# A third Strassen product taken by a second level in the second feed-forward product of a transformer layer; its weight differences made in an earlier stage

## The chip, the core and the metric

The kernel runs on one core of a Trainium2 chip. The metric is the device time of one execution in microseconds (us). A core has TensorE (PE, with its weight load PEld), VectorE (DVE), ScalarE (ACT), GpSimd (POOL), and SyncE (SP), which here issues nearly all DMA transfers. Each engine runs its instructions in the order in which the program lists them, and waits on semaphores for the others.

## What is computed

One layer of a transformer trunk, in float32, for x of 1024 x 1024 (sequence by model width), memory of 256 x 1024, and a feed-forward width of 4096. Cut to what matters:

```
h = rmsnorm(x, g_mix_pre);  proj = h @ w_in
y = concat(rmsnorm(forgetting_attention(...)), rmsnorm(chunked_relpos_attention(...)))
x = x + rmsnorm(y @ w_out, g_mix_post)
h = rmsnorm(x, g_mem_pre);  mem_n = rmsnorm(mem, g_mem_kv)
y = memory_cross_attention(h, mem_n, w_mq, w_mk, w_mv, w_mo)      # 4 heads
x = x + rmsnorm(y, g_mem_post)
h = rmsnorm(x, g_ff_pre)
y = square(relu(h @ w_ff1)) @ w_ff2                               # 1024x1024x4096, 1024x4096x1024
x = x + rmsnorm(y, g_ff_post)
```

## The kernel before

Every float32 operand is split into a high part (rounded, on ACT, `whi`, `ah`, ...) and a low part (the rest, mostly on DVE, `wlo`, `al`, ...), and every product is three matmuls: high by high, high by low, low by high. The large products use Strassen's scheme with seven products of half-size blocks, in the variant whose right-hand differences are T1 = B12 − B11, T2 = B22 − T1, T3 = B22 − B12 and T4 = T2 − B21 (the signs are carried by the sums).

The stages, by their time in the profiled execution:

- **Attention**, to about 500 us.
- **The memory attention stage**, about 500 to 816 us: the output projection of the attention, the memory queries, scores, and the product with `w_mo`. Its order is not written out: a planner (class `Flow`) takes steps for TensorE from several generators, and keeps for V (VectorE), S (ScalarE), G (GpSimd) and D (the DMA queue) a clock of its own and a list of waiting pieces, each with a cost in us and a level. A piece with a lower level goes first. "Pumps" are called ahead of each step and may put new pieces into the lists. A load is reckoned to take 4.5 us (3.5 in `Sums`) after its 0.55 us of issue. One pump, `Sums` (L1095 to L1124), already makes right-hand differences: it loads pieces of `w_mo`, forms T1 to T4 on DVE (`B11r`, `B12r`, ..., L1115) and stores them to DRAM. The order that the planner finds is the order of each engine's instructions.
- **The tail of that stage**, about 816 to 838 us, ordered by hand: the last column of the product with `w_mo` (`ym11b`), while DVE makes the last low parts `wlomo_1_2` and `wlomo_1_3` (L455) and POOL adds rows (`xf`).
- **The first feed-forward product**, to 1147.9 us: for 16 blocks j of 256 columns of the hidden layer, one Strassen level, order written out by hand. A block adds its weight pieces (`Weights.sums`, `sum4`: `sd`), splits them (`v0lo_s`, ...), runs products into the banks px, pz, pv, and turns the sums into seven left-hand matrices for the second product, stored in DRAM (`put(j, n, ...)` into `gd`). For j < 7 a first half of the block was computed in advance and is read back (`p1r`). In `if late` (0 < j < 7) the next block's weight sums are on DVE, otherwise on POOL. The matrices n = 1 and n = 5 are stored in parts (`put_parts`), and after each odd j a "form" per matrix (`put_sums`, four DVE instructions of 128x256, L1893 and on, and two stores) makes the sums S1 to S4 of a second level. The forms are made in the next block, one after `g22` (`g<-pz,u`) and one at its end.
- **The second feed-forward product**, from 1147.9 us to about 1447: Strassen with seven products n, eight "outer" steps k each. An outer step is 24 matmuls of 128x512 into four banks. n = 1 and n = 5 are taken by a second Strassen level, 14 "inner" steps each, an inner step being 24 matmuls of 128x256 (bank `fi`). n = 3 (T1) comes first, by eight outer steps into banks of its own (`fy`); then n = 0, 2, 4, 6 into `fx`, with one inner step after each outer step (and a second one at four places) until all 28 are done. So there are 68 steps. `fetch` loads a step's two operands four steps ahead, `combine` (L2186 to L2215) forms its right-hand difference on DVE, and `prepare` (L2217 to L2234) splits both operands (L2229 to L2232).

Of the kernel before, what the change touches and what calls it, by code (L numbers as in the profile page):

```python
# [14 lines left out]
F32 = mybir.dt.float32  # L15
# [120 lines left out]
def build(ctx, tc, nc, out, t):  # L136
# [119 lines left out]
    p1 = pool("p1", stack=p1s)  # L256

# [83 lines left out]
    def value_leave(g, kb, ps):  # L341
# [12 lines left out]
        if g == 0:  # L354
# [9 lines left out]
                 q=4, mp=4, pt=1, xt=2, wq=0).items()}  # L364
# [760 lines left out]

    class Rows:
# [646 lines left out]
    p2x = pool("p2x", stack=p2xs)  # L1773
    with tc.manual_schedule():
# [4 lines left out]
        flow.pumps.append(Sums().pump)  # L1779
# [17 lines left out]
    NP = FF // (2 * P)  # L1797
# [7 lines left out]
    def t2(name):  # L1805
        if region[0]:
            return pr.tile([P, HT], F32, tag="t2", bufs=9, name=name)
        return pf.tile([P, HT], F32, tag="t2", bufs=18, name=name)
# [62 lines left out]
    HQ = HT // 2  # L1871
    gi, even = {}, {}
    for n in (1, 5):
# [15 lines left out]
    def put_sums(n, j, c):  # L1889

        k, s, e = j // 2 % 4, j // 8, even.pop(n)
# [251 lines left out]

    NK = NP // 2
    W11, W12, W21, W22 = range(4)
    order = ((0, "B11"), (1, "B21"), (4, "T2"), (3, "T1"), (5, "T3"), (6, "B22"), (2, "T4"))
    inner = ("A11", "A12", "S2", "S1", "S3", "S4", "A22")
    steps, i = [(3, k) for k in range(NK)], 0
    for m, n in enumerate((0, 2, 4, 6)):
        for k in range(NK):  # L2150
            steps.append((n, k))
            for _ in range(min(28 - i, 1 + (m * NK + k in (6, 11, 14, 17)))):
                steps.append((("i", i // 14), i % 14))
                i += 1
    rows_a, rows_b, ops = {}, {}, {}
    t1, t2b = {}, {}

    def raw_b(q, k):
        r = u4(f"wg{q}_{k}_{len(rows_b)}", (P, D), F32)
        nc.sync.dma_start(r, t["w_ff2"][q, k])  # L2160
        return r

    def fetch(s):
# [4 lines left out]
        if n in (("i", 0), ("i", 1)):  # L2168
            name, h = inner[k // 2], k % 2
            nc.sync.dma_start(ra, gi[(1, 5)[n[1]], name][h].rearrange("p a b -> p (a b)"))  # L2170
            quads = {"A11": (0, 1), "A12": (2,), "S2": (3,), "S1": (), "S3": (0,), "S4": (3,), "A22": (2,)}[name]
            rows_b[s] = []
            for q in quads:
                rows_b[s].append(u4(f"wi{q}_{s}", (P, D), F32))
                nc.sync.dma_start(rows_b[s][-1], t["w_ff2q"][n[1], q, h])
# [3 lines left out]
        if name == "T1":  # L2179
            rows_b[s] = (raw_b(W12, k), raw_b(W11, k))  # L2180
        else:
            rows_b[s] = (raw_b({"B11": W11, "T2": W22, "T3": W11, "T4": W21}[name], k),)
# [3 lines left out]
    def combine(s, eng=nc.vector):  # L2186
# [3 lines left out]
        if isinstance(n, tuple):  # L2190
            name, key = inner[k // 2], ("i", k % 2)
            if name == "A11":
                t1[key] = rb[1]
                eng.tensor_sub(rb[1], rb[1], rb[0])
            elif name == "S1":
                rb = (t1.pop(key),)
            elif name == "S2":
                t2b[key] = rb[0]
                eng.tensor_sub(rb[0], rb[0], t1[key])
            elif name == "S3":  # L2200
                eng.tensor_sub(rb[0], t2b[key], rb[0])
            elif name == "A22":
                eng.tensor_sub(rb[0], rb[0], t2b[key])
        elif n == 3:
            t1[k] = rb[0]
            eng.tensor_sub(t1[k], *rb)
        elif n == 2:
            t2b[k] = t1.pop(k)
            eng.tensor_sub(t2b[k], rb[0], t2b[k])
            rb = (t2b[k],)  # L2210
        elif n == 4:
            eng.tensor_sub(rb[0], t2b[k], rb[0])
        elif n == 6:
            eng.tensor_sub(rb[0], rb[0], t2b[k])
# [20 lines left out]
    with manual:  # L2235
        sums, stores = (lambda: []), []
        for j in range(NP):
# [3 lines left out]
            late = more and 0 < j < AHEAD  # L2241
# [25 lines left out]
            forms = sums()  # L2267
# [19 lines left out]
            stores = [form() for form in forms[:1]]  # L2287
            if late:
# [25 lines left out]
            stores = [form() for form in forms[1:]]  # L2314
# [4 lines left out]
            def sums(j=j, u2=u2, u3=u3, g11=g11, g22=g22):  # L2319
# [4 lines left out]
                put(j, 3, s1)  # L2324
# [6 lines left out]
                return [lambda: put_sums(1, j, u3), lambda: put_sums(5, j, s4g)] if j % 2 else []  # L2331
# [260 lines left out]
```

## Time and profile before

| | us |
|---|---|
| Median of 3 runs | 1458.01 (1457.24 to 1458.23) |
| Profiled execution, its time | 1455.46 |
| Profiled execution, its span | 1453.7 |
| TensorE busy | 1443.0 (99%) |
| First matmul of the first feed-forward product's block loop | 880.4 |
| First matmul of the second feed-forward product | 1147.9 |

The span runs from the first to the last instruction of the profile; 1.8 us of the time lie outside it. The profile lists busy time by engine, waits by what ended them, groups of equal instructions, and single instructions with start and duration. A row of the timeline reads: start, duration, engine, line, operation, output<-inputs, shape, and in brackets the idle time ahead of it with what ended it. Rows of several instructions end in x and their count.

### The profile page before, as it was taken

The numbers are of one execution on the slowest core, as the hardware profiler recorded it, in microseconds if no ns is written. First come the engines' busy times: TensorE is split into PE (matmuls) and PEld (weight loads), VectorE is DVE, ScalarE is ACT, GpSimd is POOL, SyncE is SP. The second block draws the span as 40 slices with busy tenths as digits, with TensorE's granted clock in tenths as the row PEclk, the third lists the DMA queues.
The fourth block names the chain that finished last, engine by engine and source line by source line (L and its number), as shares of the span: only waits on it lengthen the run. The fifth ranks groups of instructions, "written<-read, shape, count | busy, mean of one in ns | idle before, by whom it ended". The sixth has DMA issues, their size and how long they took to land.

```text
span 1453.7 us, 21860 instructions
## 1 busy us (share of the span) xinstructions
PE 1443.0 (99%) x7553; PEld 1231.0 (85%) x7553; DVE 1093.1 (75%) x1854; ACT 845.1 (58%) x1465; POOL 389.1 (27%) x496
## 2 busy tenths in 40 slices
PE   9999999999999999999999999999999999999998
PEld 8988888888889888888788888888888888888886
DVE  7787777766677847976874687896666866789897
ACT  6567677666677836555553455555555545555553
POOL 1245456554455311521231411003223000000003
PEclk9999999999999999999999999999999999999999
DMA  7132324321325585552541546875545897786786
GB/s 277 49 97 71 83 64 144 86 81 48 95 58 154 175 307 181 188 177 85 178 155 44 177 154 222 278 251 182 177 167 188 309 342 247 253 281 231 278 288 204
DMA packets 104351, 255.29 MB, mean 176 GB/s; under 512 B 11673, under 2 KB 30113, under 8 KB 104241
## 3 DMA queue, kind: packets, MB, share of 16 engines
q1 hardware_dynamic: 104096, 253.65, 52.7%
q8 instruction: 59, 0.97, 0.3%
q14 instruction: 52, 0.42, 0.1%
q10 hardware_dynamic: 144, 0.26, 0.1%
HBM read 184.07 MB, written 61.40 MB: 169 GB/s over the span
## 4 chain that ended last, share of the span: by engine, by line
PE 96%; DVE 2%; ACT 1%; issue 0%; DMA 0%; SPq 0%; DVEq 0%; ACTq 0%
PE pv L754 4%; PE fx L194 4%; PE fx L193 4%; PE fx L195 4%; PE ptr L711 4%; PE px L195 3%; PE px L194 3%; PE px L193 3%; PE pz L193 2%; PE k L193 2%; PE mq L195 2%; PE q L193 2%; PE q L194 2%; PE q L195 2%; PE mq L194 2%; PE k L194 2%
## 5 line engine op out<-in xcount | busy, mean ns | idle before, releaser
L717 DVE TENSOR_TENSOR phl<-ptr,phl 128x512 fp32r<-128x512 f32 (+1 forms) x152 | 92.5, 615 | 31.6 <-ACT phl L720 30.6
L720 ACT ACTIVATE phl<-ptr 128x512 fp32r<-128x512 f32 (+1 forms) x152 | 79.7, 539 | 40.4 <-PE ptr L711 38.6
L2229 ACT ACTIVATE whif<-ra 128x1024 fp32r<-128x1024 f32 x45 | 47.6, 1058 | 77.7 <-PE fx L194 34.8
L2364 POOL TENSOR_SCALAR rf<-sf 128x1 f32<-128x1 f32 x7 | 7.0, 1001 | 315.8 <-ACT jf L2345 315.6
L754 PE MATMUL pv<-phl,vs 128*128 128x512 f32 (+1 forms) x304 | 85.2, 366 | 0.2 <-DVE phl L717 0.2
L2231 DVE TENSOR_TENSOR wlof<-ra,whif 128x1024 fp32r<-128x1024 f32 x45 | 54.9, 1221 | 36.0 <-ACT whif L2229 35.8
L193 PE MATMUL fx<-vhif,whif 128*128 128x512 f32 x168 | 65.6, 390 | 0.0
L194 PE MATMUL fx<-vlof,whif 128*128 128x512 f32 x168 | 65.6, 390 | 0.0
L195 PE MATMUL fx<-vhif,wlof 128*128 128x512 f32 x168 | 65.4, 389 | 0.0
L754 PEld LDWEIGHTS pv<-phl,vs 128*128 128x128 f32 x304 | 55.1, 188 | 11.1 <-DVE phl L717 0.8
L768 POOL TENSOR_TENSOR o<-o 64x256 f32<-64x256 f32 x64 | 47.8, 747 | 52.8 <-DVE o L766 34.4
L2080 POOL TENSOR_TENSOR sc<-wf,wf 128x512 f32<-128x512 f32 x8 | 12.7, 1589 | 176.9 <-DMA wf<-in_w_ff 163.3
L766 DVE TENSOR_TENSOR o<-pv,o 64x512 f32<-64x512 f32 x64 | 44.0, 688 | 13.6 <-ACT o L771 12.2
L193 PE MATMUL k<-hT_hi,whik 128*128 128x512 f32 x128 | 53.6, 419 | 0.0
L193 PE MATMUL q<-hT_hi,whiq 128*128 128x512 f32 x128 | 51.6, 403 | 0.0
L193 PE MATMUL mq<-h2T_hi,whimq 128*128 128x512 f32 x128 | 51.3, 401 | 0.0
L195 PE MATMUL k<-hT_hi,wlok 128*128 128x512 f32 x128 | 50.3, 393 | 0.0
L195 PE MATMUL mq<-h2T_hi,wlomq 128*128 128x512 f32 x128 | 50.1, 392 | 0.2 <-DVE wlomq L455 0.2
L194 PE MATMUL k<-hT_lo,whik 128*128 128x512 f32 x128 | 50.3, 393 | 0.0
L195 PE MATMUL q<-hT_hi,wloq 128*128 128x512 f32 x128 | 50.2, 392 | 0.0
L194 PE MATMUL q<-hT_lo,whiq 128*128 128x512 f32 x128 | 50.2, 392 | 0.0
L194 PE MATMUL mq<-h2T_lo,whimq 128*128 128x512 f32 x128 | 50.1, 392 | 0.1
(715 smaller groups left out, 5207.7 us busy)
## 6 DMA issues: line engine op xcount, KB each, us to landing
wg<-in_w_ff SPq DMA_DIRECT2D x48, 512.0 KB, 6.0
ra<-gd SPq DMA_DIRECT2D x40, 512.0 KB, 4.8
wf<-in_w_ff SPq DMA_DIRECT2D x38, 512.0 KB, 4.2
wi<-in_w_ff2q SPq DMA_DIRECT2D x28, 512.0 KB, 6.4
wrawmq<-in_w_mq SPq DMA_DIRECT2D x16, 512.0 KB, 4.1
gd<-s SPq DMA_DIRECT2D x32, 256.0 KB, 2.6
gd<-g SPq DMA_DIRECT2D x25, 256.0 KB, 2.7
wrawq<-in_w_qk SPq DMA_DIRECT2D x8, 512.0 KB, 4.6
```

The costliest lines, as they stand in the source:

```text
L193: nc.tensor.matmul(ps, lh, rh, start=start, stop=False, skip_group_check=more)
L194: nc.tensor.matmul(ps, lh, rl, start=False, stop=False, skip_group_check=more)
L195: nc.tensor.matmul(ps, ll, rh, start=False, stop=stop, skip_group_check=more)
L711: nc.tensor.transpose(tr[:, m, :], sp[:, k * P:(k + 1) * P], ident)
L717: flow.put("V", at, 0.7, lambda: nc.vector.tensor_sub(pl[:, live, :], tr[:, live, :], f(ph[:, live, :])), done)
L720: flow.put("S", flow.end, 0.6, lambda ph=ph, tr=tr, live=live: nc.scalar.activation(ph[:, live, :], tr[:, live, :], AF.Copy), split)
L754: nc.tensor.matmul(pv[:, :, qs_, :], v, hl[:, :, hs, :], start=c == 0 and turn == 0, stop=last)
L766: flow.put("V", at, 0.7, lambda: nc.vector.tensor_add(o2[own], pv[own, :, :, ::step], o2[own]), lambda end: (free["pv"].give(end), flow.pu ...
L768: free["pv"].give(end), flow.put("G", end, 0.8, lambda: nc.gpsimd.tensor_add(o2[own, 0], o2[own, 0], o2[own, 1]), store)))
L2080: eng.tensor_sub(sc[:, k1], r0[:, k0], r1[:, k0])
L2229: nc.scalar.activation(ah, ra, AF.Copy)
L2231: nc.vector.tensor_sub(al, ra, f(ah))
```

## The change

Three parts.

**In the memory attention stage** a new pump, `Ready`, works off 16 units (eight k, two column halves a) between 60 and 400 us of the planner's time after the stage's start. A unit takes four buffers of 128x512 of a new pool `pp` (eight buffers), loads one piece of each quadrant of `w_ff2`, makes four differences on DVE at level 3 (behind everything else that is ready), and stores them: T3 to `wd[4]`, T1 to `t1d`, T2 to `wd[2]`, T4 to `wd[6]`. Together 64 DVE instructions and 128 transfers of 256 KB.

**In the first feed-forward product** the matrix n = 3 is stored in parts and gets forms as n = 1 and n = 5 have. The three forms of two blocks wait in a queue: in each block one is made after `g22`, and at the end of a block half of what is left. `late` now ends one block earlier (0 < j < 6), so at j = 6 the weight sums of the next block are on POOL. The forms of the last block are made in steps 2, 4 and 6 of the second product.

**In the second feed-forward product** n = 3 is taken by 14 inner steps, ahead of those of n = 1 and n = 5. There are 32 outer and 42 inner steps, 74 in all: from the second outer step on two inner steps follow each outer one, and the last eight outer steps are alone. Outer steps load their right-hand difference ready-made (`wd`), and the inner steps of n = 3 load theirs from `t1d` in runs of 1 KB. The DVE combinations of the outer steps are gone; those of the inner steps stay.

```diff
+    START, WHEN = [], ((60, 400),)
+    class Ready:
...
+        def pump(self):
+            if self.left and free["pp"].ready(4) and any(x <= flow.now - START[0] < y for x, y in WHEN):
+                for _ in range(4):
+                    free["pp"].take()
+                self.unit(*self.left.pop(0))
+        def unit(self, k, a):
+            r, lv = {}, 3
...
+            def load(q, then):
+                flow.load(flow.now, lambda: nc.sync.dma_start(r[q], t["w_ff2"][q, k][:, cs]), then)
+            def sub(op, x, y, z):
+                return [("V", 0.6, lambda: op(r[x], r[y], r[z]))]
...
+            last = lambda at: flow.chain(at, sub(minus, W21, W21, W11), made(W21, whole(6)), lv)
+            t2_ = lambda at: flow.chain(at, sub(plus, W11, W22, W11), made(W11, whole(2), last), lv)
+            t1_ = lambda at: flow.chain(at, sub(minus, W12, W12, W11), made(W12, t1d[k // 4][:, k % 4, a], t2_), lv)
+            landed = all_of(("pp", k, a), 4, lambda at: flow.chain(at, sub(minus, W22, W22, W12), made(W22, whole(4), t1_), lv))
...
-        flow.pumps.append(Sums().pump)
+        flow.pumps += [Sums().pump, Ready().pump]
+        START.append(flow.now)
...
-    for n in (1, 5):
+    for n in (1, 5, 3):
...
-    steps, i = [(3, k) for k in range(NK)], 0
+    steps, i = [], 0
     for m, n in enumerate((0, 2, 4, 6)):
         for k in range(NK):
             steps.append((n, k))
-            for _ in range(min(28 - i, 1 + (m * NK + k in (6, 11, 14, 17)))):
-                steps.append((("i", i // 14), i % 14))
+            w = m * NK + k
+            while i < min(42, 42 * (w - 1) // 22):
+                steps.append((("i", (2, 0, 1)[i // 14]), i % 14))
                 i += 1
...
+                if n[1] < 2:
+                    nc.sync.dma_start(rows_b[s][-1], t["w_ff2q"][n[1], q, h])
+                else:
+                    nc.sync.dma_start(rows_b[s][-1].rearrange("p (a n) -> p a n", a=4),
+                                      t1d[h][:, :, q // 2, q % 2 * HQ:q % 2 * HQ + HQ])
...
+        right[s] = u4(f"wg{s}", (P, D), F32)
+        nc.sync.dma_start(right[s], t["w_ff2"][W11, k] if n == 0 else wd[n][k])
...
-            late = more and 0 < j < AHEAD
+            late = more and 0 < j < AHEAD - 1
...
-            forms = sums()
+            forms += sums()
...
             stores = [form() for form in forms[:1]]
+            del forms[:1]
...
-            stores = [form() for form in forms[1:]]
+            stores = [form() for form in forms[:len(forms) // 2]]
+            del forms[:len(forms) // 2]
...
-                put(j, 3, s1)
+                put_parts(3, j, s1)
```

What the engines' rows show. First VectorE at the end of the memory attention stage, before (L455 makes a low part, L1565 scales a row of `ym`):

```order
L455 TENSOR_TENSOR wlomo_1_0_9206<-wrawmo_1_0_9001,whimo_1_0_9205 128x1024
L455 TENSOR_TENSOR wlomo_1_1_9225<-wrawmo_1_1_9180,whimo_1_1_9224 128x1024
L1565 TENSOR_TENSOR ym_9035<-ym_9043,g_mem_post 128x512
L1565 TENSOR_TENSOR ym_9036<-ym_9051,g_mem_post 128x512
L1565 TENSOR_TENSOR ym_9037<-ym_9129,g_mem_post 128x512
L455 TENSOR_TENSOR wlomo_1_2_9261<-wrawmo_1_2_9216,whimo_1_2_9260 128x1024
L1565 TENSOR_TENSOR ym_9038<-ym_9143,g_mem_post 128x512
L455 TENSOR_TENSOR wlomo_1_3_9271<-wrawmo_1_3_9228,whimo_1_3_9270 128x1024
```

The same place in the change, where L1156 with `pp` is a unit's difference:

```order
L461 TENSOR_TENSOR wlomo_1_1_9495<-wrawmo_1_1_9429,whimo_1_1_9494 128x1024
L1156 TENSOR_TENSOR pp_71_9433<-pp_71_9433,pp_71_9431 128x512
L1156 TENSOR_TENSOR pp_71_9431<-pp_71_9431,pp_71_9432 128x512
L1156 TENSOR_TENSOR pp_71_9432<-pp_71_9433,pp_71_9432 128x512
L1614 TENSOR_TENSOR ym_9273<-ym_9281,g_mem_post 128x512
L1156 TENSOR_TENSOR pp_71_9434<-pp_71_9434,pp_71_9432 128x512
L1614 TENSOR_TENSOR ym_9274<-ym_9292,g_mem_post 128x512
L461 TENSOR_TENSOR wlomo_1_2_9536<-wrawmo_1_2_9486,whimo_1_2_9535 128x1024
L1614 TENSOR_TENSOR ym_9275<-ym_9384,g_mem_post 128x512
L1614 TENSOR_TENSOR ym_9276<-ym_9396,g_mem_post 128x512
L461 TENSOR_TENSOR wlomo_1_3_9552<-wrawmo_1_3_9498,whimo_1_3_9551 128x1024
```

The last unit's four differences now stand behind `wlomo_1_1` and ahead of `wlomo_1_2`.

Second, VectorE in block j = 5 of the first feed-forward product, before:

```order
L2282 TENSOR_TENSOR u_5_10643<-px_10583,p1r_10528 128x512
L2286 TENSOR_TENSOR g_5_10645<-pz_10614,u_5_10643 128x512
L2087 TENSOR_TENSOR sd_10647<-wf_10448,sc_10627 128x512
L1848 TENSOR_TENSOR v0lo_s_10650<-sc_10627,v0hi_s_10649 128x1024
L1848 TENSOR_TENSOR wlo_s1a_10671<-wf_10526,whi_s1a_10670 128x1024
```

And in the change (`s_33` are the tiles of the new form):

```order
L2315 TENSOR_TENSOR u_5_10945<-px_10885,p1r_10830 128x512
L2319 TENSOR_TENSOR g_5_10947<-pz_10916,u_5_10945 128x512
L1942 TENSOR_TENSOR s_33_10949<-s_2_10644,s_3_10769 128x256
L1943 TENSOR_TENSOR s_33_10949<-s_33_10949,s_2_10644 128x256
L1944 TENSOR_TENSOR s_33_10950<-s_2_10644 128x256
L1945 TENSOR_TENSOR s_33_10950<-s_3_10769,s_33_10949 128x256
L2136 TENSOR_TENSOR sd_10955<-wf_10750,sc_10929 128x512
L1898 TENSOR_TENSOR v0lo_s_10958<-sc_10929,v0hi_s_10957 128x1024
```

The four instructions of the form for n = 3 have come between `g` and the next block's `sd` and low part.

Third, the DMA issues on SP in the second feed-forward product, before (`gd` and `gi` hold left-hand matrices, `in_w_ff` and `in_w_ff2q` are the weights):

```order
L2178 DMA ra_12442<-gd_0_9276 128x1024
L2160 DMA wg_0_1_12444<-in_w_ff 128x1024
L2170 DMA ra_12479<-gi1A_9342 128x1024
L2175 DMA wi_9_12481<-in_w_ff2q 128x1024
L2175 DMA wi_9_12483<-in_w_ff2q 128x1024
```

And in the change:

```order
L2213 DMA ra_13161<-gi3S_9650 128x1024
L2221 DMA wi_18_13163<-t1d_156 128x4x256
L2225 DMA ra_13206<-gd_0_9594 128x1024
L2227 DMA wg_13208<-wd_0_132 128x1024
L2213 DMA ra_13242<-gi3S_9651 128x1024
L2221 DMA wi_20_13244<-t1d_157 128x4x256
L2213 DMA ra_13282<-gi3A_9646 128x1024
L2221 DMA wi_21_13284<-t1d_156 128x4x256
```

Two inner steps, reading `gi3` and `t1d`, now stand between two outer steps, and an outer step reads `wd`.

118 lines of the change are left out of this document (56 added, 62 removed).

## The prediction

> **What bounds the kernel now.** I read the totals and the chain first, then the waits of TensorE, then stretches of 50 us, then single rows of the three places that the change touches.
>
> ```profile
> PE 1443.0 (99%) x7553; PEld 1231.0 (85%) x7553; DVE 1093.1 (75%) x1854; ACT 845.1 (58%) x1465; POOL 389.1 (27%) x496
> PE 96%; DVE 2%; ACT 1%; issue 0%; DMA 0%; SPq 0%; DVEq 0%; ACTq 0%
> ```
>
> TensorE is busy for 99% of the span, and 96% of the chain that ended last is TensorE itself. So time is won by matmuls that go away, and lost where TensorE begins to wait. How little it waits now, from 480 us on (idle us, times, longest):
>
> ```profile
> PEld ym L193 <- ACT junk L1073: 0.9, 1, 0.9
> PEld pz L193 <- ACT v0hi_s L1845: 0.7, 2, 0.5
> PEld mq L195 <- DVE wlomq L455: 0.6, 1, 0.6
> PEld fy L194 <- DVE bl L2232: 0.3, 1, 0.3
> ```
>
> In the second feed-forward product (fy, fx, fi) the one wait is 0.3 us, at its start. Stretches (columns: window, length, busy us of PE, PEld, DVE, ACT, POOL, granted clock, DMA share, GB/s):
>
> ```profile
> 550.00:600.00 50.00, 50.00 (x238) 41.83 (x237) 39.79 (x54) 30.68 (x61) 15.04 (x18) 1.00 0.46 156
> 600.00:650.00 50.00, 49.94 (x275) 42.79 (x274) 42.53 (x66) 28.84 (x63) 16.98 (x25) 1.00 0.59 201
> 650.00:700.00 50.00, 49.57 (x249) 41.79 (x248) 32.47 (x64) 27.62 (x57) 3.83 (x8) 1.00 0.26 84
> 700.00:750.00 50.00, 49.84 (x251) 41.47 (x250) 45.08 (x61) 29.99 (x55) 21.49 (x20) 1.00 0.65 211
> 750.00:800.00 50.00, 49.94 (x266) 42.50 (x265) 21.96 (x45) 20.28 (x45) 7.02 (x13) 1.00 0.13 43
> 900.00:950.00 50.00, 50.00 (x222) 41.20 (x221) 45.19 (x71) 26.12 (x38) 0.00 (x0) 1.00 0.73 248
> 1150.00:1200.00 50.00, 50.00 (x233) 41.68 (x232) 36.61 (x39) 24.89 (x30) 0.00 (x0) 1.00 0.95 335
> 1250.00:1300.00 50.00, 50.00 (x301) 44.74 (x300) 45.14 (x45) 27.27 (x30) 0.00 (x0) 1.00 0.79 274
> ```
>
> VectorE is the engine with least to spare: 45 of 50 us at 700, 900 and 1250. POOL does nothing in the second product. The clock is 1.00 throughout.
>
> **Term 1: the matmuls of the third outer product.**
>
> ```profile
> 1147.86 0.39 PE L193 MATMUL fy<-vhif,whif 128*128 128x512 f32 x1
> 1191.55 0.39 PE L193 MATMUL fx<-vhif,whif 128*128 128x512 f32 x1
> 1196.99 0.28 PE L193 MATMUL fi<-vhif,whif 128*128 128x256 f32 x1
> 1199.86 0.40 PE L193 MATMUL fx<-bh,ah 128*128 128x512 f32 x1
> 1205.33 0.28 PE L193 MATMUL fi<-vhif,whif 128*128 128x256 f32 x1
> ```
>
> The first fy to the first fx is the whole of n=3: 43.69 us for eight outer steps (24 matmuls of 128x512 each, 0.2275 us apiece). An inner step (24 matmuls of 128x256) is 1199.86 − 1196.99 = 2.87 us, an outer one behind it 5.47 us. Fourteen inner steps take the place of eight outer ones: 14 × 2.87 = 40.18, so **−3.5 us**. Seven products instead of eight should give 12.5%; 8% is left, because a matmul of half the width costs 2.87/5.47 = 0.52 of a wide one. TensorE does nothing else there, so all of it counts if operands keep up.
>
> By the rows, then, 3.5 us. The Trainium skill, "TensorE: Matmul & The Clock Gate", section "Back-to-back issue gap", gives N/2.4 + 2.5 ns for an isolated warm matmul, 109 and 216 ns here; by it 192 × 0.216 − 336 × 0.109 = 4.9 us would go. This trace has 0.120 and 0.228 us at clock 1.00, so the measurement decides.
>
> Cover for the operands: in the new order a triple (one outer, two inner steps) lasts 5.47 + 2 × 2.87 = 11.2 us.
>
> ```profile
> L2231 DVE TENSOR_TENSOR wlof<-ra,whif 128x1024 fp32r<-128x1024 f32 x45 | 54.9, 1221 | 36.0 <-ACT whif L2229 35.8
> L2206 DVE TENSOR_TENSOR wg<-wg,wg 128x1024 f32<-128x1024 f32 x8 | 9.8, 1219 | 8.7 <-DMA wg<-in_w_ff 8.7
> ra<-gd SPq DMA_DIRECT2D x40, 512.0 KB, 4.8
> wi<-in_w_ff2q SPq DMA_DIRECT2D x28, 512.0 KB, 6.4
> ```
>
> Six splits (6 × 1.22) and 16 combines in 28 steps, so 1.14 a triple (1.4), and reads of the banks (estimate 1.3, from four of some 0.3): 10.0 of 11.2 us, a share of 0.90. That is what 1250–1300 has now (45.14 of 50) while PE is busy for all 50, because the outer combines (32 of 1.22 us) go to the memory stage. Loads: an average triple brings six of 0.52 MB, 281 GB/s, against 335 held without a wait at 1150. With two A11 steps it is 4 MB, 375 GB/s, for one triple; three buffers for the left operand let a load go out some 8 to 11 us (up to three steps) before its split, against the 4.8 to 6.4 that it takes. The 14 uses of `t1d` come in runs of 1 KB, which no row of before prices: 0 if they land like `wi` (nearest, my value), at most 0.5 us each, 7 us, if every one is late by the longest wait of that kind above, rounded up. The first read of the new matrices follows their last store by some 1.5 us of slack; taken as 0.
>
> **Term 2: one more form and its stores in the first product.**
>
> ```profile
> 945.00 0.42 DVE L1893 TENSOR_TENSOR s<-u,u 128x256 f32<-128x256 f32 x1
> 946.47 0.68 DVE L2087 TENSOR_TENSOR sd<-wf,sc 128x512 f32<-128x512 f32 x1
> 958.83 0.69 DVE L2286 TENSOR_TENSOR g<-pz,u 128x512 f32<-128x512 f32 x1
> 960.04 1.22 DVE L1848 TENSOR_TENSOR v0lo_s<-sc,v0hi_s 128x1024 fp32r<-128x1024 f32 x1
> 962.49 0.39 PE L193 MATMUL px<-T_hi,v0hi_s 128*128 128x512 f32 x1
> 965.65 0.69 DVE L2264 TENSOR_TENSOR u<-px,p1r 128x512 f32<-128x512 f32 x1 [1.46 <-DMA p1r<-p1d]
> ```
>
> A form is four instructions, 945.00 to 946.47: 1.47 us. At j=3 and j=5 the new one stands behind `g` (958.83), ahead of `sd` and `v0lo_s`. That ends at 961.26 now and 962.73 then. TensorE's first px matmul is at 962.49 and the first that reads the low half two matmuls later, 962.95: it fits by 0.2 us, and the 1.46 us that VectorE then stands before `u` takes up the rest. At odd j above 6 its `nxt.sums` is POOL's already. At j=6 four additions, 2.7 us, leave VectorE for POOL, which has none there. Four extra stores per pair of blocks ride on a DMA share of 0.73. I take **0**, between −0.4 (a wait at j=6 goes) and +1.0 (the 0.2 us is missed at 2 blocks by half a microsecond).
>
> **Term 3: 64 subtractions and 128 transfers in the memory stage.**
>
> ```profile
> 528.97 0.69 DVE L1115 TENSOR_TENSOR B11r<-B12r,B11r 128x512 f32<-128x512 f32 x1 [5.55 <-DMA B12r<-in_w_mo]
> 533.64 0.69 DVE L1115 TENSOR_TENSOR B21r<-B22r,B21r 128x512 f32<-128x512 f32 x1
> 534.24 0.68 DVE L1115 TENSOR_TENSOR B12r<-B22r,B12r 128x512 f32<-128x512 f32 x1
> 807.18 6.71 DVE L455 TENSOR_TENSOR wlomo<-wrawmo,whimo 128x1024 fp32r<-128x1024 f32 x3 [1.13 <-ACT whimo L449]
> 816.93 1.23 DVE L455 TENSOR_TENSOR wlomo<-wrawmo,whimo 128x1024 fp32r<-128x1024 f32 x1 [0.40 <-ACT whimo L449]
> 819.17 1.23 DVE L455 TENSOR_TENSOR wlomo<-wrawmo,whimo 128x1024 fp32r<-128x1024 f32 x1 [0.25 <-ACT whimo L449]
> ```
> ```profile
> 821.08 0.39 PE L194 MATMUL ym<-wlomo,oT_hi 128*128 128x512 f32 x1
> ```
> ```profile
> 804.55 11.76 POOL L1938 TENSOR_TENSOR xf<-h3T_hi,h3T_lo 128x512 f32<-128x512 f32 x7 [5.13 <-PE mo L194]
> ```
>
> Back to back such a subtraction costs 534.24 − 533.64 = 0.60 us: 64 are 39 us. From 550 to 800 VectorE is idle for 250 − 181.8 = 68 us, so they fit, and the planner gives them its last rank. But VectorE keeps its order: each can hold up the next real piece of work by what is left of it. TensorE had four places without slack (the waits above and three shorter); with one subtraction ahead of each, 4 × 0.6 = 2.4 us at most. At the end four subtractions stand ahead of the last two `wlomo`. The last ends at 820.40 and TensorE reads it at 821.08: slack 0.7 against 4 × 0.6 = 2.4, less the 1.13 + 0.40 + 0.25 us for which VectorE stands. That is 0 here; without that idle time 1.7. Beside POOL's additions a split took 6.71/3 = 2.24 instead of 1.23 us; stretched by as much, the four cost 4.4 and 4.4 us is the upper bound. I take 0.5 for each place, **+1.0 us**, near the lower bound because idle time is nearest in the rows; bounds 0 and 2.4 + 4.4 = 6.8.
>
> On that stretch: the Trainium skill, "SBUF — State Buffer", section "Who interferes with whom", says that a VectorE instruction with two SBUF inputs and a GpSimd instruction reading SBUF take one shared port by turns, each for its whole length. By it each of the four could stand 11.76/7 = 1.68 us, 6.7 in all; the rows (2.24 against 1.23) agree in direction and are milder.
>
> **Sum**: −3.5 + 0 + 1.0 = **−2.5 us**. Against the profiled execution (1455.46 us, span 1453.7, 1.8 outside it) that is 1452.96; that run lies 2.55 under the median of 1458.01, so the forecast for the median is **1455.5**.
>
> **Rivals.** What a measurement can tell here is about 0.2%, 2.9 us.
>
> A, all hidden: the first term whole, perhaps half a microsecond more from j=6 and the vanished wait at fy: −2.9 to −4.0, 1454.0 to 1455.1. For it: 68 us idle against 39, and the lowest planner rank. Against: the places without slack.
>
> B, the forecast: 0.6 to 3.4 us given back, 1455.1 to 1458.0.
>
> C, VectorE stands in the memory stage for loads that the planner thinks landed. It counts 4.5 us; a unit of just this kind stood 5.55 us at 528.97, and the same kind of load took this long:
>
> ```profile
> B11r<-in_w_mo SPq DMA_DIRECT2D x4, 256.0 KB, 7.0
> ```
>
> That is 2.5 us late, so a unit costs 4 × 0.6 + 2.5 = 4.9 us. Sixteen in 250 us put 6.4 into 600–650 and 700–750: 31.6 us against 12.4 idle there, 19 too many; if half drifts to the emptier neighbours, some 9 us reach TensorE. −3.5 + 9 = +5.5: 1463.5, slower. It decides from 6.4 us lost. Against: what is held up is mostly work made in advance.
>
> D, the change doesn't do what it says: `t1d` and the doubled traffic are late in the second product, +7 − 3.5 = +3.5, 1461.5.
>
> **Chances.** A 0.36, B 0.40, C 0.19 (0.04 of it ending within 0.2%), D 0.05. So faster 0.36, within 0.2% 0.44, slower 0.15 + 0.05 = 0.20. The likeliest case, B, spans 1455.1 to 1458.0; the range takes in most of A and C to where half of its loss arrives, D's price among it: 1453.8 to 1461.5.
>
> **What would show it.** Term 1: from the first matmul of the second product to its last, 3.5 us less, and no wait on `wi` or `ra` above 0.5 us; a wait there on `t1d`'s rows means D. Term 2: block starts 13.6 us apart at j=3 to 6 as now. Term 3: the first `px` of the first product at the same time or up to 3.4 us later; VectorE rows of `pp` with idle time ended by a load of several microseconds, and TensorE waiting on what follows, mean C. The forecast is wrong if the first product starts over 4 us later, or if an inner step in the new triples takes more than 2.9 us.

## The result and the profile after

The changed kernel takes 1468.39 us (median of 6 runs, 1466.07 to 1470.14) against 1457.69 for the kernel before (6 runs), a ratio of 1.0074, 95% interval 1.0061 to 1.0087: **slower by 10.7 us**, outside the stated range. The profiled execution took 1468.09 us, its span is 1466.0. Totals of the page (engine, busy us, share of the span, instructions):

```profile
PE 1444.9 (99%) x7697; PEld 1235.4 (84%) x7697; DVE 1132.4 (77%) x1948; ACT 857.1 (58%) x1481; POOL 398.2 (27%) x500
```

TensorE is still busy for 99%, so the totals show nothing of the loss. The five largest waits of PE from 480 us on do (what waits, for what, us in total, times, longest):

```profile
PE pz L193 <- DVE g L2319: 4.2, 4, 3.1
PE fi L194 <- DVE vlof L2265: 1.6, 2, 1.0
PE px L195 <- DVE wlo_a L1898: 1.3, 2, 0.8
PE px L193 <- ACT whi_a L1895: 1.1, 1, 1.1
PE ym L194 <- DVE wlomo L461: 0.7, 1, 0.7
```

Only `fi`, the first inner steps of the second product, is work that the change added; the others are `g` of the first product and the way out of the memory attention stage (`wlo_a`, `whi_a`, `wlomo`). The same stretches as before (columns as there):

```profile
600.00:650.00 50.00, 49.67 (x272) 42.63 (x271) 46.45 (x72) 30.09 (x64) 17.45 (x27) 1.00 0.70 246
750.00:800.00 50.00, 49.91 (x272) 42.60 (x271) 39.30 (x75) 21.58 (x48) 7.64 (x12) 1.00 0.86 279
950.00:1000.00 50.00, 46.00 (x192) 36.35 (x191) 42.32 (x62) 23.15 (x34) 12.08 (x8) 0.97 0.70 239
1150.00:1200.00 50.00, 48.96 (x254) 41.75 (x253) 36.13 (x49) 25.64 (x33) 0.00 (x0) 1.00 0.92 312
1250.00:1300.00 50.00, 50.00 (x315) 45.32 (x313) 40.25 (x43) 28.08 (x32) 0.00 (x0) 1.00 0.79 285
```

The 64 differences hide where they were feared, between 600 and 800 us. 950 to 1000 loses 4 us and, alone of these stretches, a piece of the clock. To place the loss, the span is cut at three matmuls of TensorE. Their rows in the changed kernel (duration min/median/max in ns, then first and last start):

```profile
L2008 PE MATMUL trx<-ident,ym x32: 270/272/331, 841.3 to 869.1; 128*128 128x128 f32 x32
L193 PE MATMUL px<-T_hi,v0hi_s x64: 389/389/504, 886.7 to 1136.4; 128*128 128x512 f32 x64
L193 PE MATMUL fx<-vhif,whif x136: 389/389/398, 1161.5 to 1457.3; 128*128 128x512 f32 x136
```

The memory attention stage is counted from the first matmul of its first product `mv` to the first `trx`; the way out from there to the first `px`; the first product from there to the first matmul of the second (`fy` before, `fx` after); the second from there to the last start of `fx<-vhif,whif`. With the experiments (us, one profile each; last column: medians of the timed runs against the kernel before in the same job):

| kernel | stage | way out | first product | second product | sum against before | timed |
|---|---|---|---|---|---|---|
| before | 351.6 | 41.9 | 267.5 | 296.8 | | |
| changed | 353.2 | 45.4 | 274.8 | 295.8 | +11.4 | +10.7 |
| r1 | 353.2 | 45.6 | 270.7 | 295.2 | +6.9 | +6.5 |
| r2 | 353.9 | 45.3 | 269.5 | 294.9 | +5.8 | +5.5 |
| r3 | 354.4 | 45.4 | 268.1 | 295.1 | +5.2 | +5.2 |
| r4 | 353.1 | 47.0 | 268.5 | 296.6 | +7.4 | +5.7 |
| r5 | 355.4 | 42.7 | 268.1 | 295.5 | +3.9 | +3.6 |
| r6 | 376.8 | 42.0 | 268.1 | 295.3 | +24.4 | +25.1 |
| r7 | 353.1 | 46.6 | 268.1 | 293.5 | +3.5 | +3.4 |
| r8 | 378.2 | 41.9 | 268.2 | 293.4 | +24.0 | +23.5 |
| r9 | 369.4 | 41.9 | 268.2 | 293.4 | +15.1 | +14.8 |
| r10 | 354.9 | 42.9 | 268.2 | 293.4 | +1.6 | +1.4 |
| r11 | 371.7 | 42.3 | 268.1 | 293.7 | +17.9 | +14.4 |
| r12 | 351.9 | 41.7 | 268.1 | 298.9 | +2.8 | +3.6 |
| r13 | 352.2 | 41.7 | 268.8 | 293.4 | -1.7 | -1.8 |
| r14 | 352.4 | 41.7 | 266.9 | 293.4 | -3.4 | -2.5 |

So of the change's 11.4 us, 7.3 are lost in the first product, 5.1 in the stage and its way out, and the second product wins 1.0 where 3.5 were worked out. (The two profiled executions differ by 1.2 us more ahead of `mv`, from 9 us on, in work that is the same in both; the medians don't show it. r11's profiled execution is 2.8 us above its median.)

**The first product.** Its blocks j = 3 to 6 last 14.62, 14.56, 14.74 and 24.20 us (13.75, 13.60, 13.93 and 19.45 before). VectorE in block j = 5, whose first px is at 956.67, and what SP issues behind it:

```profile
969.80 0.69 DVE L2136 TENSOR_TENSOR sd<-wf,sc 128x512 f32<-128x512 f32 x1
976.18 0.69 DVE L2297 TENSOR_TENSOR u<-px,p1r 128x512 f32<-128x512 f32 x1 [1.63 <-DMA p1r<-p1d]
```
```profile
970.51 0.33 SPq L1883 DMA_DIRECT2D wf<-in_w_ff  x1
970.90 0.42 SPq L2151 DMA_DIRECT2D p1r<-p1d  x1
```

`sd` ends at 970.49; only then is the buffer of the next `wf` free, and SP issues that load at 970.51. The load of `p1r` stands behind it on the same queue, so it goes out 14.2 us into the block. Before, where the block's first px was at 948.56, it went out 12.0 us into it:

```profile
960.53 0.42 SPq L2102 DMA_DIRECT2D p1r<-p1d  x1
```

`u` of the next block waits for this load, and the next matmuls into px wait for `u`. Then block 6, on VectorE, POOL and TensorE:

```profile
976.79 1.14 DVE L2358 TENSOR_TENSOR s<-u,g 128x512 f32<-128x512 f32 x1
977.97 1.67 DVE L2360 TENSOR_TENSOR u<-p1r,u 128x512 f32<-128x512 f32 x1
979.56 1.78 DVE L2362 TENSOR_TENSOR s<-s,p1r 128x512 f32<-128x512 f32 x1
983.12 1.22 DVE L1898 TENSOR_TENSOR v1lo_s<-sc,v1hi_s 128x1024 fp32r<-128x1024 f32 x1
984.97 0.69 DVE L2319 TENSOR_TENSOR g<-pz,u 128x512 f32<-128x512 f32 x1
```
```profile
977.46 1.63 POOL L2131 TENSOR_TENSOR sc<-wf,wf 128x512 f32<-128x512 f32 x1
979.17 1.62 POOL L2136 TENSOR_TENSOR sd<-wf,sc 128x512 f32<-128x512 f32 x1
```
```profile
982.32 0.39 PE L195 MATMUL pv<-T_hi,wlo_s1a 128*128 128x512 f32 x1
985.81 0.77 PE L193 MATMUL pz<-B_hi,u0hi_s 128*128 128x512 f32 x1 [3.10 <-DVE g L2319]
987.23 0.63 PE L193 MATMUL pz<-B_hi,u0hi_s 128*128 128x512 f32 x1
```

Three additions of 0.69 us take 1.14, 1.67 and 1.78 while POOL adds, and where `late` is off the split `v1lo_s` (1.22 us) stands ahead of `g`, not behind it. `g` comes late, TensorE stands 3.1 us, and then its matmuls follow one another every 0.43 us instead of 0.23 for three microseconds more.

**The way out of the stage.** POOL and VectorE:

```profile
815.99 13.29 POOL L1987 TENSOR_TENSOR xf<-h3T_hi,h3T_lo 128x512 f32<-128x512 f32 x7 [14.18 <-PE ym L195]
```
```profile
813.36 2.14 DVE L1156 TENSOR_TENSOR pp<-pp,pp 128x512 f32<-128x512 f32 x3 [0.74 <-DMA t1d<-pp]
817.35 1.73 DVE L1156 TENSOR_TENSOR pp<-pp,pp 128x512 f32<-128x512 f32 x1
819.60 1.71 DVE L461 TENSOR_TENSOR wlomo<-wrawmo,whimo 128x1024 fp32r<-128x1024 f32 x1
822.43 1.21 DVE L461 TENSOR_TENSOR wlomo<-wrawmo,whimo 128x1024 fp32r<-128x1024 f32 x1
```

The last four differences stand where the order had them and the last `wlomo` ends at 823.6 instead of 820.4. That was foreseen. TensorE, compared matmul by matmul from `mv` on, is 0.4 us later than in the kernel before at 818 us, and 1.6 us later once its wait for `wlomo` (0.7 us, at 823) is over: most of what the stage's row lost is lost here, at its end. What was not foreseen: POOL's seven `xf` begin at 816.0 instead of 804.6, so the row norms behind them on POOL come some 6 us later (1.2 of them the later `mv`), and the transposes `trx` come late too. Until 829 us POOL now also adds beside VectorE's last difference (1.73 us) and the next `wlomo` (1.71). In the program the second `xf` waits, besides TensorE's work, for the last units' differences and stores: its tile lies over the buffers of `pp`. The row names TensorE alone; r5 tests it.

**The second product.** VectorE and SP near its start:

```profile
1183.98 1.23 DVE L2238 TENSOR_TENSOR wi<-wi,wi 128x1024 f32<-128x1024 f32 x1 [6.38 <-DMA wi<-t1d]
```
```profile
1171.83 0.52 SPq L1936 DMA_DIRECT2D gi3A<-s  x1
1175.16 1.25 SPq L2221 DMA_DIRECT2D wi<-t1d  x2
```

The loads for step 5 are issued at 1175 behind stores of the last block's sums, which wait for VectorE.

### The profile page after: what moved, and what is told of

It reads as the page before. It is cut to its first block, busy times and chain, and to the rows that moved or that the text cites. A ratio compares the mean times of both kernels' runs of the same rounds, so it can differ in the third digit from the quotient of the medians.

```text
span 1466.0 us, 22556 instructions
## 1 busy us (share of the span) xinstructions
PE 1444.9 (99%) x7697; PEld 1235.4 (84%) x7697; DVE 1132.4 (77%) x1948; ACT 857.1 (58%) x1481; POOL 398.2 (27%) x500
## 5 line engine op out<-in xcount | busy, mean ns | idle before, releaser
L2262 ACT ACTIVATE whif<-ra 128x1024 fp32r<-128x1024 f32 x49 | 52.0, 1061 | 88.2 <-PE fx L194 32.1
L2264 DVE TENSOR_TENSOR wlof<-ra,whif 128x1024 fp32r<-128x1024 f32 x49 | 59.9, 1222 | 35.3 <-ACT whif L2262 35.0
L194 PE MATMUL fi<-vlof,whif 128*128 128x256 f32 x256 | 72.6, 284 | 1.6 <-DVE vlof L2265 1.6
L195 PE MATMUL fi<-vhif,wlof 128*128 128x256 f32 x256 | 72.4, 283 | 0.0
L193 PE MATMUL fi<-vhif,whif 128*128 128x256 f32 x256 | 72.4, 283 | 0.0
L772 DVE TENSOR_TENSOR o<-pv,o 64x512 f32<-64x512 f32 x64 | 44.0, 688 | 13.5 <-ACT o L777 12.1
L193 PE MATMUL fx<-vhif,whif 128*128 128x512 f32 x136 | 53.1, 390 | 0.0
L194 PE MATMUL fx<-vlof,whif 128*128 128x512 f32 x136 | 53.0, 390 | 0.0
L195 PE MATMUL fx<-vhif,wlof 128*128 128x512 f32 x136 | 52.9, 389 | 0.0
L194 PEld LDWEIGHTS fi<-vlof,whif 128*128 128x128 f32 x256 | 49.1, 192 | 2.5 <-DVE vlof L2265 2.1
```

Source lines behind the costliest of these rows:

```text
L193: nc.tensor.matmul(ps, lh, rh, start=start, stop=False, skip_group_check=more)
L194: nc.tensor.matmul(ps, lh, rl, start=False, stop=False, skip_group_check=more)
L195: nc.tensor.matmul(ps, ll, rh, start=False, stop=stop, skip_group_check=more)
L772: flow.put("V", at, 0.7, lambda: nc.vector.tensor_add(o2[own], pv[own, :, :, ::step], o2[own]), lambda end: (free["pv"].give(end), flow.pu ...
L2262: nc.scalar.activation(ah, ra, AF.Copy)
L2264: nc.vector.tensor_sub(al, ra, f(ah))
```

## The experiments

### r1: late as before

```diff
-            late = more and 0 < j < AHEAD - 1
+            late = more and 0 < j < AHEAD
```

> The changed kernel with late = 0 < j < 7 again, so at j = 6 the next block's weight sums are on VectorE as before; all else as changed. In the changed kernel block j = 6 lasted 24.20 us against 19.45, with TensorE waiting 3.3 us on g. Theory P (POOL's sums run beside VectorE's four additions s, u, s, s, which took 5.2 instead of 2.65 us, and the low half of v now stands ahead of g): with the sums back on VectorE the four take 2.7 us again, g comes 13.56 - 2.5 - 1.1 + 2.1 = 12.0 us into the block, the wait shrinks to about 1.7 us, and the time falls by 1.6 to 2.9 us, to 1465.5 to 1466.8. Rival (only the late load of p1r matters at j = 6, and POOL relieved VectorE): 2.1 us of sums come back onto VectorE ahead of g, block 6 gets longer by about 1 us, the time rises to 1469.4.

Measured: 1463.01 us, ratio to before 1.0047 (1.0034 to 1.0060). Block 6 lasts 21.36 us.

```profile
975.18 0.68 DVE L2358 TENSOR_TENSOR s<-u,g 128x512 f32<-128x512 f32 x1
975.90 0.69 DVE L2360 TENSOR_TENSOR u<-p1r,u 128x512 f32<-128x512 f32 x1
976.50 0.69 DVE L2362 TENSOR_TENSOR s<-s,p1r 128x512 f32<-128x512 f32 x1
981.74 0.69 DVE L2319 TENSOR_TENSOR g<-pz,u 128x512 f32<-128x512 f32 x1
```

The additions are back at 0.69 us and `g` comes 12.2 us into the block (969.50) instead of 13.6, as theory P had it; the clock stays at 1.00. Moving 2.1 us of sums off VectorE had made the block 2.8 us longer. By the rows the stretched additions cost 2.5 us ahead of `g` and the split 1.1; the edit undoes both at once. Against the kernel before the time fell by 4.2 us, more than expected, but 1.0 of it was not argued: block 3, which the edit doesn't touch, lasted 13.62 us in this profile, because its `p1r` had landed within 5.2 us of its issue and not in 6.3. Why it landed sooner is not shown.

### r2: the form behind the splits

```diff
-            stores = [form() for form in forms[:1]]
-            del forms[:1]
             if late:
                 nxt.sum4(nc.vector)
             if late or more and not j:
                 nxt.split("s23")
+            stores = [form() for form in forms[:1]]
+            del forms[:1]
```

> The changed kernel with the form in a block's middle made behind the next block's sd and the split of v, not ahead of them; late as changed. Theory Q (the form delays sd, sd frees the weight buffer, and the next weight load and the load of p1r behind it on SP go out late, so u of the next block is late, and this carries on from block to block): p1r is asked for about 12 us into a block again, blocks 3, 4 and 5 last 13.6 to 13.9 instead of 14.6, and block 6 gains 1.5 us too: the time falls by 4 to 5.5 us, to 1463 to 1464.4. Rival (VectorE has 1.5 us too much to do in these blocks, wherever the form stands): the blocks stay at 14.4 to 14.7 us and the time within 0.5 us of 1468.4.

Measured: 1462.09 us, ratio 1.0042 (1.0030 to 1.0055). `p1r` is asked for 11.4 to 12.1 us into the block, blocks 3 to 5 last 13.61, 13.59 and 14.04 us, block 6 21.52. Theory Q holds: VectorE has the same to do in these blocks, and only the order differs.

### r3: both

> Both edits together: form behind the splits, and late = 0 < j < 7. If theories P and Q hold and nothing else is late in the first product, its blocks last what they did before (267.5 us from the first px to the second product, against 274.8), and the time falls by 7.3 us, to about 1461.1. If the two losses are one and the same (only the late p1r), the result is that of r2 or worse. What is left above the kernel before (about 3.4 us) is then the memory stage and its way out.

Measured: 1461.72 us, ratio 1.0034 (1.0021 to 1.0046). The first product lasts 268.1 us, 0.6 more than before: 6.7 of its 7.3 us are explained, and the two losses are two, though they overlap: block 6 lasts 24.20 us in the changed kernel, 21.36 and 21.52 with one edit, 20.19 with both. The time is 5.2 us above before, not 3.4. The stage's code is that of the changed kernel, but TensorE waited 1.8 us for `wlomo` at 825 us where it had waited 0.7; why the same order is later in one profile than in another is not shown.

### r4: the stage's part alone, in the kernel before

The kernel before with `Ready`, `pp` and the stores added; nothing reads what they make.

> The kernel before with the change's part in the memory attention stage alone: the 64 differences, 64 loads and 64 stores are made, and nothing reads them. Theory T (the loss of this part is at the stage's way out: POOL's seven xf additions began at 816.0 instead of 804.6 us, the chain of row norms behind them came later, and TensorE waited at 824, 842, 862 and 881 us, 4.8 us in all): 1457.7 + 4.8 = 1462.5, with the first px of the first product 4 to 5 us later than before, and no more waits on TensorE from 550 to 800 us than before. Rival (the differences are hidden, and the later start belongs to the profiled executions' first microseconds, which differ by 1.2 us, and to the first product's edits): 1457.7 to 1459.

Measured: 1462.26 us, ratio 1.0040 (1.0026 to 1.0053): 5.7 us against the expected 4.8. Stage and way out are longer by 1.5 and 5.1 us, and TensorE's waits between 600 and 800 us are within 0.3 us of those of before. The loss is this part's own. Some 1.6 of the 5.1 us go with a stretch of half clock in this profile (0.50 from 863.8 to 867.2 us); without them the sum is +5.8, close to the +5.7 of the timed runs. (The first product, untouched here, lost 1.0 us: `p1r` landed 0.9 us later behind block 5. It stands on an edge.)

### r5: pp's buffers elsewhere

```diff
-    p2x = pool("p2x", stack=p2xs)
     pp = pool("pp", stack=p2xs)
+    p2x = pool("p2x", stack=p2xs)
```

on r3.

> r3 (form behind the splits, late as before) with the pool pp opened ahead of p2x, not behind it, so that POOL's xf tiles no longer lie over the pp buffers; the order of the 64 differences is the same. Theory M (the second xf waits for the last units' stores and differences because it lies over their buffers, so POOL's seven additions come 11 us late and the chain of row norms behind them 5): POOL starts them 10 us or more earlier, the stretch from the first trx to the first px of the first product shrinks from 45.4 to about 42 us, and r3's 5.2 us above the kernel before become about 1.7. Rival (the four last differences stand ahead of the last low parts and of the ym rows on VectorE, whatever POOL does): the stretch stays at 45 us and the time at 5 above before.

Measured: 1459.87 us, ratio 1.0022 (1.0013 to 1.0031). The way out is 42.7 us, as theory M has it, but the stage became 1 us longer than in r3, and 1.6 of the 3.5 us came back. POOL now runs early, beside the differences:

```profile
801.45 15.21 POOL L1987 TENSOR_TENSOR xf<-h3T_hi,h3T_lo 128x512 f32<-128x512 f32 x8
```
```profile
804.78 6.28 DVE L1156 TENSOR_TENSOR pp<-pp,pp 128x512 f32<-128x512 f32 x4
810.99 2.31 DVE L461 TENSOR_TENSOR wlomo<-wrawmo,whimo 128x1024 fp32r<-128x1024 f32 x1
```

Four differences take 1.57 us each instead of 0.60, a split 2.31 instead of 1.23. The wait became a contention: M was half of it. Here the Trainium skill, "SBUF — State Buffer", section "Who interferes with whom", fits the row: a VectorE instruction with two SBUF inputs and a GpSimd one that reads SBUF take turns at a shared port. Each of the four took some 1.0 us longer than alone; by that section the prediction had 1.68 us of standing for each, so the row agrees in kind and is milder.

### r6 and r8: the units earlier

r6 is r3 with `WHEN = ((20, 400),)`, r8 the same on r7.

> r3 with the window of the units opened at 20 us of the planner's time, not 60: the last unit is then done well ahead of the stage's end, no difference stands among the last low parts, and no store of a unit is under way when POOL's xf begin. Theory M and its rival both expect the way out of the stage as before: trx and the first px 2.8 and 3.5 us earlier, 1.1 us faster than the kernel before in all (-3.5 + 1.7 of waits in the second product, +0.7 in the first). A third theory (64 differences and 33 MB of traffic cost TensorE somewhere in the stage wherever they stand): the waits move to 520 to 560 us, where VectorE already stood 5.6 us for a load of w_mo, and the time stays 2 us or more above before.

> All four edits: form behind the splits, late as before, units from 20 us on, loads of step 5 ahead of the last block's sums. If the losses are separate and found, the time is that of the kernel before less 3.5 us for the third product, plus some 0.7 us that the first product's blocks 5 and 6 still lose and 0.4 us of waits: 2.4 us below the kernel before. If not, it shows what is left.

Measured: r6 1481.38 us, ratio 1.0171 (1.0157 to 1.0185); r8 1479.77, ratio 1.0159 (1.0145 to 1.0173). The way out is as before (42.0 and 41.9 us), and the stage is 25 and 27 us longer, by the third theory and far beyond its price; r8's expected 2.4 us below the kernel before were missed by as much. VectorE, SP and TensorE in r6:

```profile
570.01 0.69 DVE L1156 TENSOR_TENSOR pp<-pp,pp 128x512 f32<-128x512 f32 x1 [11.03 <-DMA pp<-in_w_ff]
```
```profile
563.64 2.27 SPq L1153 DMA_DIRECT2D pp<-in_w_ff  x4
```
```profile
PE ssh L1065 <- DVE sq L1025: 15.2, 1, 15.2
```

In the planner's order the load had landed; in the run it had not, VectorE stood 11 us in its order, and TensorE 15. This is the prediction's rival C, at another place and by another cause: C had loads that land slowly, but here no load of a unit took more than 6.9 us in this stretch. The one waited for was issued late, at 563.6, behind the stores of the units before it. It did not happen in the changed kernel, whose window opens 40 us later: there VectorE stood 0.9 us for the units' loads in the whole stage.

### r7: loads first

```diff
-            if s == 1:
-                forms = sums()
             stores = [forms.pop()()] if s in (2, 4, 6) else []
...
             if s + 4 < len(steps):
                 fetch(s + 4)
+            if s == 1:
+                forms = sums()
```

on r3.

> r3 with the loads for step 5 of the second product issued ahead of the last block's sums (and their stores, which stand on the same queue and wait for VectorE), not behind them. In r3 VectorE stood 5.6 us for the loads of t1d that were issued behind these stores, and TensorE lost 1.6 us between 1150 and 1200 us. Theory S (the loads are late because they are issued late, behind stores that wait): VectorE's 5.6 us shrink below 1 us, TensorE loses 0.3 us or less there, and the time falls by 1.3 us to 3.9 above before. Rival (t1d's runs of 1 KB land late however early they are asked for): the wait stays within a microsecond and the time within 0.5 us of r3.

Measured: 1459.66 us, ratio 1.0021 (1.0012 to 1.0030): 1.8 us less than r3. The second product lasts 293.5 us:

```profile
L193 PE MATMUL fx<-vhif,whif x136: 389/389/397, 1155.6 to 1449.1; 128*128 128x512 f32 x136
```

Theory S holds, and the 3.5 us are there: 296.8 − 293.5 = 3.3. VectorE's wait for the loads of step 5 is gone (5.6 us in r3). That runs of 1 KB are slow is refuted by the landing times in the changed kernel, the same for `t1d` and for whole rows:

```profile
wi<-in_w_ff2q SPq DMA_DIRECT2D x28, 512.0 KB, 6.1
wi<-t1d SPq DMA_DIRECT2D x14, 512.0 KB, 6.0
```

### r9, r10, r11: the units ahead, and the buffers elsewhere, on r7

r9: `r, lv = {}, 1`. r10: r7 with r5's edit. r11: r9 with r5's edit.

> r7 (form behind the splits, late as before, loads first) with the units' differences at level 1, not 3, so the planner places them ahead of the other chains on VectorE; the window still opens at 60 us. The last difference is then placed 35 instructions ahead of the last low part wlomo, and POOL's second xf waits for nothing that is new. Theory (the stage costs only at its way out): the way out is as before, 5 us are won against r7's 3.4 above the kernel before, and the time is 1.6 to 1.8 us below it. Rival (a difference ahead of a chain that TensorE waits for costs 0.6 us at each such place, four known ones, and VectorE stands for late loads as it did in r6): up to 2.4 us of new waits between 590 and 790 us and more where a load is late, so 0.6 us or more above the kernel before.

> r5 and r7 together: pp's buffers ahead of p2x, and the loads of step 5 ahead of the last block's sums; the units at level 3. If the two gains are separate (1.6 and 1.8 us in 5.2): 1.8 us above the kernel before. In r5 POOL's xf ran beside the last differences and low parts on VectorE, and TensorE lost 3.5 us from 800 to 850 us; that stays.

> r9 with pp's buffers ahead of p2x. If with the units out of the way nothing at the way out hangs on their buffers, this is r9 within 0.5 us; if POOL's xf, which can then start earlier, run beside VectorE's low parts and stretch them (2.2 instead of 1.2 us for a split, as in the kernel before at 807 us), TensorE loses about 1 us from 800 to 850 us, and this is 1 us slower than r9.

Measured: r9 1471.45 us, ratio 1.0104 (1.0088 to 1.0119); r10 1458.09, ratio 1.0010 (1.0001 to 1.0018); r11 1471.06, ratio 1.0102 (1.0089 to 1.0116). r10 adds up: 1.4 us above before, 1.8 expected. r9's theory is half right, the way out is 41.9 us, but the stage is 16 us longer than in r7, over three times the 4.7 us that the way out won back. The waits are:

```profile
PE ym L195 <- DVE S4o L1418: 5.9, 1, 5.9
PE tr_h2T L1291 <- DVE yw L1212: 4.6, 2, 2.7
```

They are at 610 and 727 us, in two of the stretches where VectorE had least to spare, and the granted clock was 0.50 from 609.9 to 616.7 and from 722.5 to 732.8 us. The rival had the places, and priced them too low. Late loads were not it: VectorE stood 0.8 us for them. Level 3 was what kept the differences cheap. r11 is r9 within 0.4 us: with no unit at the end, the time doesn't hang on the buffers.

### r12: the last units by hand

Units 13 to 16 are made in the first product (r7 otherwise):

```diff
+            if j in (7, 9, 11, 13):
+                k, a = NK - 2 + (j - 7) // 4, (j - 7) // 2 % 2
...
+                for q in r:
+                    nc.sync.dma_start(r[q], t["w_ff2"][q, k][:, cs])
...
+            if j in (8, 10, 12, 14):
+                r, k, a, cs = byhand
+                nc.vector.tensor_sub(r[W22], r[W22], r[W12])
...
```

> r7 (form behind the splits, late as before, loads first) with the last four of the 16 units taken out of the memory stage and made by hand in the first product's blocks 7 to 14: loads at the start of an odd block, the four differences at the start of the next one, where VectorE stands 3.8 us, and the stores behind them. The stage's last difference is then done some 40 us before its end, and the order of VectorE ahead of ym, wlomo and POOL's xf is that of the kernel before. Theory (at the stage's way out it is the last units that cost, by their place on VectorE and by their buffers): trx and the first px are as early as before, the blocks from 7 on stay at 19.04 us, and 5 us are won against r7's 3.4 above the kernel before: 1.6 to 1.9 us below it. Rival (the 12 units that stay, or their traffic, cost there too; or the by-hand units bring waits of their own into blocks 7 to 14): at or above the kernel before.

Measured: 1459.95 us, ratio 1.0025 (1.0016 to 1.0035). Stage and way out are 351.9 and 41.7 us, as before, so it is the last units that cost there. But the second product lost 5 us at its start: SP issued the fourth unit's stores from 1135.6 on, the operands of step 1 came behind them, and TensorE waited 2.1 us at 1152 us, with a stretch of half clock after it. So the rival's second half came true, a little further on.

### r13 and r14: three by hand; the form at the block's end

r13 is r12 with blocks 7, 9 and 11 only, and 13 units in the stage. r14 adds

```diff
-            stores = [form() for form in forms[:1]]
-            del forms[:1]
+            m = 0 if j % 2 and j < AHEAD else 1
+            stores = [form() for form in forms[:m]]
+            del forms[:m]
...
-            stores = [form() for form in forms[:len(forms) // 2]]
-            del forms[:len(forms) // 2]
+            m = max(len(forms) // 2, 1 - m)
+            stores = [form() for form in forms[:m]]
+            del forms[:m]
```

> As r12 with three units by hand (blocks 7 to 12) and 13 in the memory stage. In r12 the way out was as before, but TensorE lost 5 us at the start of the second product, 2.3 of them at 1152 us, behind the fourth by-hand unit, whose differences and stores stood in block 14. Theory (all of the change's loss above its 3.5 us is in the places found: blocks 3 to 6, the way out, the start of the second product): with the fourth unit back in the stage the way out stays as before, the second product starts as in r7, and the time is 1.5 to 2.3 us below the kernel before. Rival (part of the 3.5 us was never there: the new order of the second product costs that much more elsewhere): at the kernel before or above it, with no wait of TensorE to account for it.

> r13 with the odd blocks' form (below block 7) made at the block's end, where VectorE stands for p1r, not in its middle. In r3 and all after it block 6 still lasted 20.2 us against 19.45: the form of block 5 pushed u0lo_s and u back by 1.5 us, the ReLU of u and the four sums of block 6 came 0.8 us later, and g with them. Theory: block 6 lasts 19.5 us and the time falls by another 0.5 to 0.8 us, to 2.2 to 3 us below the kernel before. Rival (the form at the end delays u<-px,p1r of the next block by as much): block 6 stays at 20.2 us.

Measured: r13 1454.65 us, ratio 0.9986 (0.9977 to 0.9995); r14 **1453.90 us, ratio 0.9981 (0.9972 to 0.9990)**, 2.5 us faster than the kernel before. Both theories hold: r13 is 1.8 us below the kernel before, and block 6 lasts 19.28 us in r14. That r14 ends at the −2.5 us of the forecast is chance: it is another order of work. All waits of PE from 480 us on:

```profile
PE mq L194 <- DVE h2T_lo L1298: 0.3, 1, 0.3
PE yw L193 <- ACT yw L1247: 0.3, 1, 0.3
PE ym L193 <- DVE ym L1565: 0.2, 1, 0.2
PE pv L760 <- DVE phl L723: 0.2, 1, 0.2
```

## Why the prediction was wrong, point by point

- **What bounds the kernel**: right. What was lost or won is waits, matmuls and stretches of half clock of TensorE.
- **Term 1, −3.5 us**: the matmuls are right (−3.4 us in r9, r10, r13 and r14), the cover only in part. The rates held (VectorE 40.25 of 50 us from 1250 on, loads landing in 6 us), but "three buffers for the left operand let a load go out some 8 to 11 us (up to three steps) before its split" took the buffers for the only condition. At the start the load stands on SP behind stores that wait for VectorE. −1.0 was left of −3.5; of the 2.4 us between, r7 got 1.6 to 1.8 back by the order of issue alone, and 0.7 had come back with r3's edits to the first product. Rival D had the place, late operands of the inner steps, but its price was hung on runs of 1 KB, which cost nothing.
- **Term 2, taken as 0, +1.0 at most; measured +7.3.** This is the step that failed, in the sentence "it fits by 0.2 us, and the 1.46 us that VectorE then stands before `u` takes up the rest". That idle time was no reserve. It ends with the load of `p1r`, which is issued behind the load that `sd` releases; what delays `sd` moves the end of the idle time as well. The form was costed on VectorE alone, and the queue behind it left out (2.6 us in blocks 3 to 5, by r2). The other half, "At j=6 four additions, 2.7 us, leave VectorE for POOL", counted them as taken away; in fact they stretched VectorE's own additions and put a split ahead of `g` (block 6, and r1). Term 2 is not the whole of the miss: with the first product mended the time was still 5.2 us above before (r3).
- **Term 3, +1.0 within 0 to 6.8; measured +5.1.** In the stage up to 818 us 0.4, close to nothing, as the idle time promised. The place at the end was right and its size too small, in part because of a wait that the prediction did not list: `xf` lies over the new buffers (r5). The bound on the whole held; the 4.4 us for the last four differences would not have held beside POOL, where four took 6.28 us (r5). Its sign of being wrong, a first `px` over 4 us late, came: 886.7 against 880.4 us.
- **Rivals**: C was priced for the stage and did not happen there in the changed kernel; r6 shows VectorE standing for a load as C feared, though for a late issue and not a slow landing. (In C's price 6.4 × 4.9 is 31.4, not 31.6; nothing hangs on it.) A and B needed term 2 at 0.
- **The chances**: 0.20 for slower came from terms 1 and 3 alone. Term 2 had a range of 1.4 us around nothing and no rival of its own.

Not settled: why TensorE's wait for `wlomo` differs between profiles of the same code in the stage (0.2 us in r7, 0.7 in the changed kernel, 1.8 in r3), how the 5.1 us divide between the differences ahead of `wlomo` and the late `xf`, since moving one moved the other, and how block 6's loss divides between the stretched additions and the split.

## What to carry to other kernels

Idle time ahead of an instruction is a reserve only if what ends it does not itself depend on the instruction that is to be delayed: follow the release back, through the buffer that it frees and the queue that its load stands in, before counting on it. A new pool's buffers are waited for by whatever is laid over them later, and an addition moved to POOL may come back as a longer one on VectorE, as here from 0.69 to 1.78 us. A change that loses in four places may still be right: here its own term was there in full, and the losses were places in an order, which could be mended one by one.

## What the runs showed of the hardware

After TensorE stood 3.1 us (changed kernel, to 985.8) its granted clock was half for 3.4 us. Twelve matmuls took 4.3 us instead of 2.7, so the wait cost 1.6 us more than itself:

```profile
987.00:989.00 2.00, 2.00 (x6) 1.52 (x6) 2.00 (x4) 0.62 (x2) 1.49 (x1) 0.50 0.43 139
```

How long the wait was does not settle whether this happens. In r12 the clock was 0.50 from 1153.4 to 1156.7 after a wait of 2.1 us, and in r4 from 863.8 to 867.2 after two waits of 1.1 and 0.5 us; in r2 it stayed at 1.00 after 2.2 us, in r1 after 1.5. What else decides is not shown. A 128x512 addition on VectorE with both inputs in SBUF took up to 1.78 us beside POOL's additions, and 0.69 alone.
